# Four edits to a gated delta rule beside a stream of fp32 matmuls: a shorter inversion on VectorE, decay masks ahead of the exponential, two scalings given to ScalarE

## The chip, the cores and the metric

One core of a Trainium2 chip. The metric is the device time of one execution in microseconds (us); the time before is the median of three runs, 1537.29 us (1536.48 to 1538.0). The kernel's engines appear under the names of the profile: PE is TensorE (PEld its weight loads), DVE is VectorE, ACT is ScalarE, POOL is GpSimd, SP is the engine whose queue issues most transfers.

## The reference, cut to what matters

One decoder layer on 256 tokens of width 2048, all in fp32. After an RMSNorm, one wide input projection makes q, k, v, z, gates and a pooled branch. The part that the change touches is the gated delta rule, with 16 heads of 128 columns:

```
g = cumsum(g);  decay[i,j] = exp(g_i - g_j) for j <= i, else 0
lmat = strictly lower part of (beta_i k_i . k_j) * decay;  amat = lmat + I
u, w = solve(amat, [beta v, beta k exp(g)])        # unit lower triangular
o = (q decayed) . state + ((q . k) * decay) . (u - w . state);  state updated per chunk
o = rmsnorm(o) * gdn_norm_w * silu(z)
mixed = sigmoid(g_a) * o + sigmoid(g_b) * y_b;  x = x + mixed @ w_out
```

After that follow another RMSNorm, a gated MLP with a causal convolution (width 5632), a residual and a final RMSNorm. The kernel takes chunks of 128 tokens, two of them (t = 0, 1), in place of the reference's 64; the result is the same function.

## The kernel before, in words

**The weight stream.** Nearly all time goes into products of 256 tokens with weights that come from HBM in pieces of 128x1024 fp32 (512 KB). Each piece is loaded by SP into one of four `raw` buffers, rounded to fp32r by ACT (`whi`, line 317, in `begin`), and its rest is made by DVE (`wlo = raw - whi`, line 328). Three buffers each hold `whi` and `wlo`; `weights()` asks for pieces two ahead (`AHEAD = 2`). In `gemm_a` (lines 365 to 367) each piece feeds 12 matmuls: three products (high by high, low by high, high by low) for two 128-row parts and two token halves. So ACT, DVE and PE each run in a fixed order of their own; a late cast or split holds PE, and a PE that still reads an old piece holds the next cast.

**The groups.** The heads are worked in four groups g of four heads. For each group PE does the projections k, q, v, pool input, gate b, z, gate a and a small pool product. Beside them runs the delta rule of the group, `gdn` (lines 860 to 1093), a Python generator: `side()` is called after each 6 matmuls of a gemm and advances it by one `yield`, so that its instructions are emitted between those of the gemm. A scheduler then orders the instructions of each engine by its own model of their times; `tc.issue_after` adds an order, and inside `manual_schedule` PE keeps exactly the order of emission. Such a block (`fixed_order`) begins with the fourth group's gate a, and the small matmuls of its delta rule start behind six of the eight pieces there (`ending`); the block lasts through the first 12 pieces of the output projection.

**Inside `gdn`**, in order:

- `crow` (lines 871 to 874): the cumulated log decays of four heads as rows, brought to all 128 partitions by a DMA. `differences` (line 879): for each head and chunk one DVE instruction subtracts the partition's own value (`cumc`) and takes the minimum with 0. ACT takes the exponential (line 888, two heads at once), and POOL clears the entries below the diagonal (`affine_select`, line 890). The result is `dec0`, `dec1`.
- Grams (lines 901 to 925): for two heads at a time PE makes k.k and q.k products in PSUM (`pg0`, `pg1`); DVE takes the norms from the diagonal (line 906) and writes the products, scaled by `sj` and the decays, to `ga0` and `ga1`; the half of `pg0` that belongs to the next chunk is scaled by `sj` and `tail` (line 923).
- The inversion (lines 957 to 976): the 32x32 diagonal blocks of `lmat` go through DRAM (`cdd`, lines 939 and 942) so that 128 partitions hold 32 blocks times four parts `cq`; the inverse `tb` is 8 columns per partition (`idb` is the identity cut that way, line 635). For j = 0 to 30 DVE multiplies column j of the block by entry j of all 8 columns (line 965) and subtracts (line 967), over rows j+1 to 31. The result goes back through DRAM (`tbd`, written at line 972 and read at line 975) into `TTa`, and DVE transposes it (line 987). Larger blocks are built by small matmuls (line 1011 on).
- Output: w, the state and the outputs `po[0]` (PSUM) and `po[1]` (line 1079, in `vt`), their mean squares (lines 1085 and 1086), and the factor `ro` (lines 1088 to 1091, with a power on POOL).

**`gated`** (lines 1208 to 1216), after `gdn`: DVE multiplies both outputs by the gate `sz` (line 1211, 128x512 each), then eight instructions of 128x128 scale by `ro` and add `yb` (line 1215). `mixed` turns `sz` on PE (line 410) and makes `mhi` and `mlo` for the output projection. For groups 0 to 2 the scheduler places these transposes; for group 3 (`end`, after line 1240) they stand at a fixed place: four `side()` calls, so 24 matmuls, behind the point where `gated` is emitted.

Of the kernel before, what the change touches and what calls it, by code (L numbers as in the profile page):

```python
# [27 lines left out]
B0 = 32  # L28
NR = P // B0
AHEAD = 2  # L30
WAIT = 5
LATE = (26, 24, 22, 18)


@with_exitstack
def kernel(
# [20 lines left out]
    nc = tc.nc  # L57
# [5 lines left out]
    dpool = ctx.enter_context(tc.tile_pool(name="dram", bufs=2, space=bass.MemoryType.DRAM))  # L63
# [5 lines left out]
    def nm(s):  # L69
        cnt[0] += 1  # L70
        return f"{s}_{cnt[0]}"
# [561 lines left out]
    for cq in range(4):  # L633
        pr = slice(32 * cq, 32 * cq + 32)
        nc.gpsimd.affine_select(idb[pr], ones[pr, 0:1].unsqueeze(2).to_broadcast([32, 8, B0]),
                                pattern=[[-1, 8], [1, B0]], compare_op=ALU.is_equal, fill=0.0, base=-8 * cq,
                                channel_multiplier=0)


# [69 lines left out]
    nc.vector.tensor_scalar(mid, tri, tri[:, 63:64], None, op0=ALU.subtract)  # L709
    crs = mp.tile([NH, 2, P], F32, name="crs")  # L710
    crd = dpool.tile([4, 4 * S], F32, tag="crd", bufs=1, name="crd")
    cumc = mp.tile([P, 2, NH], F32, name="cumc")
    tail = mp.tile([P, NH], F32, name="tail")
    head = mp.tile([P, NH], F32, name="head")
    nhead = mp.tile([P, NH], F32, name="nhead")
# [1 line left out]
    def running_sums():  # L717
        pcr = pg([NH, 2, P])
        for t in range(2):
            mm(pcr[:, t, :], glog[:, t, :], mid, start=True, stop=True)  # L720
        nc.vector.tensor_copy(crs, pcr)
        nc.sync.dma_start(crd.rearrange("g (h s) -> (g h) s", h=4), crs.rearrange("h t i -> h (t i)"))
        yield
        pcc = pg([P, 2, NH])
        for t in range(2):
            nc.tensor.transpose(pcc[:, t, :], crs[:, t, :], ident[:NH, :NH])
        nc.vector.tensor_copy(cumc, pcc)

# [131 lines left out]
    def gdn(g, kq, vt, conv, res):  # L860
# [3 lines left out]
        ssk = mp.tile([P, 2, 4], F32, tag="ssk", name=nm("ssk"))  # L864
        nk = mp.tile([P, 2, 4], F32, tag="nk", name=nm("nk"))
        sj = mp.tile([P, 2, 4], F32, tag="sj", name=nm("sj"))
        dec0 = mp.tile([P, 4, P], F32, tag="dec0", name=nm("dec0"))
        dec1 = mp.tile([P, 4, P], F32, tag="dec1", name=nm("dec1"))

# [3 lines left out]
            nc.sync.dma_start(crow.rearrange("p h t i -> p (h t i)"), crd[g].partition_broadcast(P))  # L873
        yield

        def differences(hp):
            for h in (2 * hp, 2 * hp + 1):
                for t in range(2):
                    nc.vector.tensor_scalar(crow[:, h, t, :], crow[:, h, t, :],
                                            cumc[:, t, 4 * g + h : 4 * g + h + 1], 0.0,  # L880
                                            op0=ALU.subtract, op1=ALU.min)

        differences(0)
        yield
        for hp in range(2):
            hs = slice(2 * hp, 2 * hp + 2)
            for t, dec in ((0, dec0), (1, dec1)):
                nc.scalar.activation(dec[:, hs, :], crow[:, hs, t, :], AF.Exp)
            for d in (dec0[:, hs, :], dec1[:, hs, :]):
                nc.gpsimd.affine_select(d, d, pattern=[[0, 2], [1, P]], compare_op=ALU.is_ge, fill=0.0, base=0,  # L890
                                        channel_multiplier=-1)
            if hp == 0:
                differences(1)
            yield
        for hp in range(2):
            h0 = 2 * hp
# [14 lines left out]
            nc.gpsimd.tensor_tensor(nk[:, :, hs], ssk[:, :, hs], half.to_broadcast([P, 2, 2]), op=ALU.pow)  # L911
            nc.vector.reciprocal(sj[:, :, hs], ssk[:, :, hs])
            nc.vector.tensor_tensor(sj[:, :, hs], sj[:, :, hs], beta[:, :, 4 * g + h0 : 4 * g + h0 + 2], op=ALU.mult)
            for h in (h0, h0 + 1):
                pg0, pg1 = grams[h - h0]
                own, next_half = slice(0, P), slice(P, S)
                hh = 4 * g + h
                ga0h = ga0[:, h, :].rearrange("p (a s) -> p a s", a=2)
                pg0h = pg0.rearrange("p (a s) -> p a s", a=2)
                nc.vector.scalar_tensor_tensor(ga0h[:, :, own], pg0h[:, :, own], sj[:, 0, h : h + 1],  # L920
                                               dec0[:, h, :].unsqueeze(1).to_broadcast([P, 2, P]),
                                               op0=ALU.mult, op1=ALU.mult)
                nc.vector.tensor_scalar(ga0h[:, :, next_half], pg0h[:, :, next_half], sj[:, 0, h : h + 1],
                                        tail[:, hh : hh + 1], op0=ALU.mult, op1=ALU.mult)
                nc.vector.scalar_tensor_tensor(ga1[:, h, :].rearrange("p (a s) -> p a s", a=2),
                                               pg1, sj[:, 1, h : h + 1],
                                               dec1[:, h, :].unsqueeze(1).to_broadcast([P, 2, P]),
                                               op0=ALU.mult, op1=ALU.mult)
                yield
# [31 lines left out]
        with tc.issue_after(last_split[0]):  # L961
            nc.vector.tensor_copy(tb, idb)
        for j in range(B0 - 1):
            tv = tmp[:, :, j + 1 :]
            nc.vector.tensor_tensor(tv, lb[:, j, j + 1 :].unsqueeze(1).to_broadcast([P, 8, B0 - 1 - j]),
                                    tb[:, :, j : j + 1].to_broadcast([P, 8, B0 - 1 - j]), op=ALU.mult)
            nc.vector.tensor_tensor(tb[:, :, j + 1 :], tb[:, :, j + 1 :], tv, op=ALU.subtract)
            if j % 3 == 2:
                yield
        tbd = dpool.tile([32, 4, 8 * B0], F32, tag="tbd", name=nm("tbd"))  # L970
        for cq in range(4):
            nc.sync.dma_start(tbd[:, cq], tb[32 * cq : 32 * cq + 32].rearrange("p c i -> p (c i)"))
        for r in range(NR):
            rs = slice(B0 * r, B0 * (r + 1))
            nc.sync.dma_start(TTa[rs, :, rs], tbd.rearrange("(q r) a (c i) -> r (a c) q i", q=8, i=B0)[r])
        yield

        for _ in conv:
# [111 lines left out]
        for t in range(2):  # L1090
            nc.vector.tensor_scalar(ro[:, t, :], ro[:, t, :], rsq[:, t : t + 1], None, op0=ALU.mult)
        yield
        res.append((po, ro))

    for g in range(4):
        kq = mp.tile([P, 4, 2, S], F32, tag="kq", bufs=1, name=nm("kq"))
# [14 lines left out]
        res = []  # L1111
# [94 lines left out]
        nc.vector.tensor_tensor(sz4, sz4, gwb.unsqueeze(1).to_broadcast([P, 8, P]), op=ALU.mult)  # L1206

        def gated(sz=sz, res=res, yb=yb):
            po, ro = res[0]
            for t in range(2):  # L1210
                nc.vector.tensor_tensor(sz[:, t, :], po[t].rearrange("p h d -> p (h d)"), sz[:, t, :], op=ALU.mult)
            for t in range(2):
                for h in range(4):
                    hs = slice(h * P, (h + 1) * P)
                    nc.vector.scalar_tensor_tensor(sz[:, t, hs], sz[:, t, hs], ro[:, t, h : h + 1], yb[:, t, hs],
                                                   op0=ALU.mult, op1=ALU.add)

        if g < 3:
            drain()
# [518 lines left out]
```

## Time and profile before

| what | value |
|---|---|
| runs | 1538.0, 1536.48, 1537.29 us; median 1537.29 |
| span of the profiled execution | 1536.8 us, mean granted TensorE clock 0.998 |
| mixer stage (groups 0 to 3) | about 50 to 766 us of the span |
| gated MLP and final norm | from there to the end |
| 512 KB weight pieces loaded by SP from `w_in` | 224, median 4.3 us from issue to landing |

A row of the profile's groups gives line, engine, operation, output and inputs, shape, count, then busy us, the mean ns of one instruction, and the engine's idle time just ahead of it with what ended it. A row of the timeline gives start, duration in us, engine, line and a count where several are merged. Successive instructions of one engine overlap by part of their duration. A matmul of 512 columns is drawn 0.39 us long, while the next begins after 0.23 us.

### The profile page before, as it was taken

How to read it: one execution, taken by the hardware profiler on the slowest of the kernel's cores; microseconds unless marked ns; L12 is line 12 of the kernel's file. 1: busy time of each engine (PE TensorE's matmuls, PEld its weight loads, DVE VectorE, ACT ScalarE, POOL GpSimd, SP SyncE). 2: the span in 40 equal slices, each digit the busy share in tenths (PEclk: the TensorE clock that was granted, in tenths of full speed). 3: DMA queues.
4: the chain of work that ended last, by engine and by line, in shares of the span. 5: the costliest groups of instructions: out<-in, count | busy, mean ns of one | idle time of the engine just before them, and what ended most of it. 6: DMA issues, size and time to landing. Idle time of an engine off the chain costs nothing. (4 is left out here: it accounts for less than half of the span.)

```text
span 1536.8 us, 20233 instructions
## 1 busy us (share of the span) xinstructions
PE 1524.3 (99%) x7290; PEld 1255.4 (82%) x7290; DVE 1268.3 (83%) x1793; ACT 853.1 (56%) x1070; POOL 80.9 (5%) x105
## 2 busy tenths in 40 slices
PE   9999999999999999999999999999999999999997
PEld 8887888787878888788888888788888888888876
DVE  6788859896589858887567899999999886889896
ACT  6455446454455445454455666666666665555553
POOL 1010002000100000000000000000000011010200
PEclk9999999999999999999999999999999999999999
DMA  8776757776576766776588556656457478566662
GB/s 276 209 229 198 203 165 207 218 216 185 148 250 201 208 169 194 231 195 186 171 263 305 179 178 219 219 206 206 154 165 243 127 238 266 172 223 207 235 201 98
DMA packets 166515, 313.62 MB, mean 204 GB/s; under 512 B 19554, under 2 KB 23426, under 8 KB 166286
## 3 DMA queue, kind: packets, MB, share of 16 engines
q1 hardware_dynamic: 157280, 283.17, 59.2%
q0 software_dynamic: 7344, 27.27, 5.5%
q10 hardware_dynamic: 1790, 1.89, 0.4%
q8 instruction: 57, 0.93, 0.3%
q14 instruction: 44, 0.36, 0.1%
HBM read 303.33 MB, written 8.95 MB: 203 GB/s over the span
## 5 line engine op out<-in xcount | busy, mean ns | idle before, releaser
L317 ACT CAST whi<-raw 128x1024 fp32r<-128x1024 f32 x420 | 441.2, 1052 | 427.1 <-PE psm L366 270.0
L328 DVE TENSOR_TENSOR wlo<-raw,whi 128x1024 fp32r<-128x1024 f32 x418 | 507.7, 1220 | 146.0 <-ACT whi L317 140.2
L317 ACT CAST whi<-quad 128x1024 fp32r<-128x1024 f32 x182 | 190.5, 1053 | 136.8 <-PE psg L1418 43.5
L328 DVE TENSOR_TENSOR wlo<-quad,whi 128x1024 fp32r<-128x1024 f32 x182 | 220.0, 1219 | 30.0 <-ACT whi L317 29.4
L367 PE MATMUL psm<-wlo,xhl 128*128 128x512 f32 x432 | 169.5, 393 | 1.3 <-DVE wlo L328 1.2
L365 PE MATMUL psm<-whi,xhl 128*128 128x512 f32 x432 | 169.0, 391 | 0.0
L366 PE MATMUL psm<-whi,xhl 128*128 128x512 f32 x432 | 168.6, 390 | 0.0
L1418 PE MATMUL psg<-whi,fhl 128*128 128x512 f32 x504 | 127.2, 390 | 0.0
L1418 PEld LDWEIGHTS psg<-whi,fhl 128*128 128x128 f32 x504 | 94.5, 188 | 19.6
L367 PEld LDWEIGHTS psm<-wlo,xhl 128*128 128x128 f32 x432 | 81.1, 188 | 18.8 <-DVE wlo L328 2.2
L366 PEld LDWEIGHTS psm<-whi,xhl 128*128 128x128 f32 x432 | 81.1, 188 | 16.8
L365 PEld LDWEIGHTS psm<-whi,xhl 128*128 128x128 f32 x432 | 81.1, 188 | 16.7
L244 DVE TENSOR_TENSOR quad<-quad,quad 128x1024 f32<-128x1024 f32 x72 | 87.6, 1216 | 0.0
L1418 PE MATMUL psg<-wlo,fhl 128*128 128x512 f32 x252 | 69.9, 389 | 0.0
L1418 PE MATMUL psg<-whi,ups 128*128 128x512 f32 x216 | 58.9, 394 | 0.0
L1418 PEld LDWEIGHTS psg<-wlo,fhl 128*128 128x128 f32 x252 | 47.3, 188 | 9.9
L1403 PE MATMUL psm<-whi,hhi 128*128 128x512 f32 (+1 forms) x140 | 54.5, 389 | 0.1
L1403 PE MATMUL psm<-whi,hlo 128*128 128x512 f32 (+1 forms) x140 | 54.1, 386 | 0.0
L1403 PE MATMUL psm<-wlo,hhi 128*128 128x512 f32 (+1 forms) x140 | 54.0, 387 | 0.0
L365 PE MATMUL psm<-whi,mhi 128*128 128x512 f32 x128 | 50.8, 397 | 0.0
L367 PE MATMUL psm<-wlo,mhi 128*128 128x512 f32 x128 | 50.0, 390 | 0.0
L366 PE MATMUL psm<-whi,mlo 128*128 128x512 f32 x128 | 49.9, 390 | 0.0
(435 smaller groups left out, 2953.7 us busy)
## 6 DMA issues: line engine op xcount, KB each, us to landing
raw<-in_w_in_dram SPq DMA_DIRECT2D x224, 512.0 KB, 4.3
raw<-in_w_up_dram SPq DMA_DIRECT2D x104, 512.0 KB, 4.8
quad<-in_w_up_dram SPq DMA_DIRECT2D x72, 512.0 KB, 5.0
raw<-in_w_down_dram SPq DMA_DIRECT2D x56, 512.0 KB, 5.1
raw<-in_w_out_dram SPq DMA_DIRECT2D x32, 512.0 KB, 4.2
quad<-in_w_down_dram POOLq DMA_DIRECT2D x32, 512.0 KB, 5.3
mv<-vrow SPq DMA_DIRECT2D x12, 512.0 KB, 4.8
taps<-in_conv_qkv_w_dram SPq DMA_DIRECT2D x16, 256.0 KB, 6.6
```

Of the source, the lines that this page charges most:

```text
L244: nc.vector.tensor_tensor(out_, plus_, minus_, op=ALU.subtract)
L317: last_cast[0] = nc.scalar.copy(hi, raw).ins
L328: last_split[0] = nc.vector.tensor_tensor(lo, raw, hi.bitcast(F32), op=ALU.subtract).ins
L365: mm(ps[:, t, :], lh(k, t), hi[:, kk, :], start=(k == 0), stop=False)
L366: mm(ps[:, t, :], ll(k, t), hi[:, kk, :], start=False, stop=False)
L367: mm(ps[:, t, :], lh(k, t), lo[:, kk, :], start=False, stop=(k == nk - 1))
L1403: mm(ps[:, cs], lhs(kk), part_[:, kk, cs], start=(first and kk == 0 and n == 0), stop=(last and kk == 1 and n == 2), skip_group_check=shared)
L1418: mm(ps, lhs(kk), w[n][:, kk], start=(first and n == 0 and kk == 0 and lhs is high), stop=False, skip_group_check=True)
```

## The change

Four edits, all in the mixer stage:

1. **Inversion.** The columns of the inverse are spread over the four parts in another way: column 4m + cq instead of 8cq + m. Before step j only columns up to j are non-zero, so the two DVE instructions of step j take n = j // 4 + 1 of the 8 columns instead of all. `tbd` is laid out anew, `[32, 8, 4, 32]`; each of its four writes now has 256 pieces of 128 bytes where it had 32 of 1024 bytes; reads keep pieces of 128 bytes.
2. **Decays.** The eight DVE subtractions of `differences` go. POOL sets the masked entries of `crow` to -1e30 (`later_rows`, one select of 128x512 for two heads) ahead of the exponential, and ACT subtracts inside the exponential through its bias (`ncum`, the negative of `cumc`), one instruction for each head and chunk: eight of 128x128 instead of four of 128x256. The four selects of 128x256 behind the exponential go.
3. **Grams.** The next-chunk half of `pg0` is scaled by ACT instead of DVE, by `st` = `sj` * `tail`, which DVE makes for two heads at once.
4. **Output norm.** In `gated` ACT scales the outputs by `ro`, eight instructions of 128x128 into `vt`; then DVE multiplies by `sz` and adds `yb`, one instruction of 128x1024 each.

```
+NEVER = -1e30
...
-                                pattern=[[-1, 8], [1, B0]], compare_op=ALU.is_equal, fill=0.0, base=-8 * cq,
+                                pattern=[[-4, 8], [1, B0]], compare_op=ALU.is_equal, fill=0.0, base=-cq,
...
-        nc.vector.tensor_copy(cumc, pcc)
+        nc.vector.tensor_scalar(ncum, pcc, -1.0, None, op0=ALU.mult)
...
-        def differences(hp):
-            for h in (2 * hp, 2 * hp + 1):
-                for t in range(2):
-                    nc.vector.tensor_scalar(crow[:, h, t, :], crow[:, h, t, :],
-                                            cumc[:, t, 4 * g + h : 4 * g + h + 1], 0.0,
-                                            op0=ALU.subtract, op1=ALU.min)
+        def later_rows(hp):
+            d = crow[:, 2 * hp : 2 * hp + 2].rearrange("p h t i -> p (h t) i")
+            nc.gpsimd.affine_select(d, d, pattern=[[0, 4], [1, P]], compare_op=ALU.is_ge, fill=NEVER, base=0,
+                                    channel_multiplier=-1)
...
-            for t, dec in ((0, dec0), (1, dec1)):
-                nc.scalar.activation(dec[:, hs, :], crow[:, hs, t, :], AF.Exp)
-            for d in (dec0[:, hs, :], dec1[:, hs, :]):
-                nc.gpsimd.affine_select(d, d, pattern=[[0, 2], [1, P]], compare_op=ALU.is_ge, fill=0.0, base=0,
-                                        channel_multiplier=-1)
+            for h in (2 * hp, 2 * hp + 1):
+                for t, dec in ((0, dec0), (1, dec1)):
+                    nc.scalar.activation(dec[:, h, :], crow[:, h, t, :], AF.Exp,
+                                         bias=ncum[:, t, 4 * g + h : 4 * g + h + 1])
...
+            nc.vector.tensor_tensor(st[:, hs], sj[:, 0, hs], tail[:, 4 * g + h0 : 4 * g + h0 + 2], op=ALU.mult)
...
-                nc.vector.tensor_scalar(ga0h[:, :, next_half], pg0h[:, :, next_half], sj[:, 0, h : h + 1],
-                                        tail[:, hh : hh + 1], op0=ALU.mult, op1=ALU.mult)
+                nc.scalar.activation(ga0h[:, :, next_half], pg0h[:, :, next_half], AF.Copy, scale=st[:, h : h + 1])
...
-            tv = tmp[:, :, j + 1 :]
-            nc.vector.tensor_tensor(tv, lb[:, j, j + 1 :].unsqueeze(1).to_broadcast([P, 8, B0 - 1 - j]),
-                                    tb[:, :, j : j + 1].to_broadcast([P, 8, B0 - 1 - j]), op=ALU.mult)
-            nc.vector.tensor_tensor(tb[:, :, j + 1 :], tb[:, :, j + 1 :], tv, op=ALU.subtract)
+            n = j // 4 + 1
+            tv = tmp[:, :n, j + 1 :]
+            nc.vector.tensor_tensor(tv, lb[:, j, j + 1 :].unsqueeze(1).to_broadcast([P, n, B0 - 1 - j]),
+                                    tb[:, :n, j : j + 1].to_broadcast([P, n, B0 - 1 - j]), op=ALU.mult)
+            nc.vector.tensor_tensor(tb[:, :n, j + 1 :], tb[:, :n, j + 1 :], tv, op=ALU.subtract)
...
-        tbd = dpool.tile([32, 4, 8 * B0], F32, tag="tbd", name=nm("tbd"))
+        tbd = dpool.tile([32, 8, 4, B0], F32, tag="tbd", name=nm("tbd"))
         for cq in range(4):
-            nc.sync.dma_start(tbd[:, cq], tb[32 * cq : 32 * cq + 32].rearrange("p c i -> p (c i)"))
+            nc.sync.dma_start(tbd[:, :, cq, :], tb[32 * cq : 32 * cq + 32])
...
-            for t in range(2):
-                nc.vector.tensor_tensor(sz[:, t, :], po[t].rearrange("p h d -> p (h d)"), sz[:, t, :], op=ALU.mult)
             for t in range(2):
                 for h in range(4):
-                    hs = slice(h * P, (h + 1) * P)
-                    nc.vector.scalar_tensor_tensor(sz[:, t, hs], sz[:, t, hs], ro[:, t, h : h + 1], yb[:, t, hs],
-                                                   op0=ALU.mult, op1=ALU.add)
+                    nc.scalar.activation(vt[:, t, h, :], po[t][:, h, :], AF.Copy, scale=ro[:, t, h : h + 1])
+            nc.vector.tensor_tensor(sz, sz, vt.rearrange("p t h d -> p t (h d)"), op=ALU.mult)
+            nc.vector.tensor_tensor(sz, sz, yb, op=ALU.add)
```

More of the change, by code (lines that the diff above doesn't have):

```diff
@@ L711 @@
     crd = dpool.tile([4, 4 * S], F32, tag="crd", bufs=1, name="crd")
-    cumc = mp.tile([P, 2, NH], F32, name="cumc")
+    ncum = mp.tile([P, 2, NH], F32, name="ncum")
     tail = mp.tile([P, NH], F32, name="tail")
@@ L866, in gdn @@
         sj = mp.tile([P, 2, 4], F32, tag="sj", name=nm("sj"))
+        st = mp.tile([P, 4], F32, tag="st", name=nm("st"))
         dec0 = mp.tile([P, 4, P], F32, tag="dec0", name=nm("dec0"))
@@ L874, in gdn @@
         yield
-        def differences(hp):
-            for h in (2 * hp, 2 * hp + 1):
-                for t in range(2):
-                    nc.vector.tensor_scalar(crow[:, h, t, :], crow[:, h, t, :],
-                                            cumc[:, t, 4 * g + h : 4 * g + h + 1], 0.0,
-                                            op0=ALU.subtract, op1=ALU.min)
-        differences(0)
+        def later_rows(hp):
+            d = crow[:, 2 * hp : 2 * hp + 2].rearrange("p h t i -> p (h t) i")
+            nc.gpsimd.affine_select(d, d, pattern=[[0, 4], [1, P]], compare_op=ALU.is_ge, fill=NEVER, base=0,
+                                    channel_multiplier=-1)
+        later_rows(0)
         yield
         for hp in range(2):
-            hs = slice(2 * hp, 2 * hp + 2)
-            for t, dec in ((0, dec0), (1, dec1)):
-                nc.scalar.activation(dec[:, hs, :], crow[:, hs, t, :], AF.Exp)
-            for d in (dec0[:, hs, :], dec1[:, hs, :]):
-                nc.gpsimd.affine_select(d, d, pattern=[[0, 2], [1, P]], compare_op=ALU.is_ge, fill=0.0, base=0,
-                                        channel_multiplier=-1)
+            for h in (2 * hp, 2 * hp + 1):
+                for t, dec in ((0, dec0), (1, dec1)):
+                    nc.scalar.activation(dec[:, h, :], crow[:, h, t, :], AF.Exp,
+                                         bias=ncum[:, t, 4 * g + h : 4 * g + h + 1])
             if hp == 0:
-                differences(1)
+                later_rows(1)
             yield
@@ L916, in gdn @@
                 own, next_half = slice(0, P), slice(P, S)
-                hh = 4 * g + h
                 ga0h = ga0[:, h, :].rearrange("p (a s) -> p a s", a=2)
@@ L963, in gdn @@
         for j in range(B0 - 1):
-            tv = tmp[:, :, j + 1 :]
-            nc.vector.tensor_tensor(tv, lb[:, j, j + 1 :].unsqueeze(1).to_broadcast([P, 8, B0 - 1 - j]),
-                                    tb[:, :, j : j + 1].to_broadcast([P, 8, B0 - 1 - j]), op=ALU.mult)
-            nc.vector.tensor_tensor(tb[:, :, j + 1 :], tb[:, :, j + 1 :], tv, op=ALU.subtract)
+            n = j // 4 + 1
[3 more added lines that the diff above has]
+            nc.vector.tensor_tensor(tb[:, :n, j + 1 :], tb[:, :n, j + 1 :], tv, op=ALU.subtract)
             if j % 3 == 2:
                 yield
-        tbd = dpool.tile([32, 4, 8 * B0], F32, tag="tbd", name=nm("tbd"))
+        tbd = dpool.tile([32, 8, 4, B0], F32, tag="tbd", name=nm("tbd"))
         for cq in range(4):
-            nc.sync.dma_start(tbd[:, cq], tb[32 * cq : 32 * cq + 32].rearrange("p c i -> p (c i)"))
+            nc.sync.dma_start(tbd[:, :, cq, :], tb[32 * cq : 32 * cq + 32])
         for r in range(NR):
             rs = slice(B0 * r, B0 * (r + 1))
-            nc.sync.dma_start(TTa[rs, :, rs], tbd.rearrange("(q r) a (c i) -> r (a c) q i", q=8, i=B0)[r])
+            nc.sync.dma_start(TTa[rs, :, rs], tbd.rearrange("(q r) m a i -> r (m a) q i", q=8)[r])
         yield
@@ L1092, in gdn @@
         yield
-        res.append((po, ro))
+        res.append((po, ro, vt))
     for g in range(4):
@@ L1208, in gated @@
         def gated(sz=sz, res=res, yb=yb):
-            po, ro = res[0]
-            for t in range(2):
-                nc.vector.tensor_tensor(sz[:, t, :], po[t].rearrange("p h d -> p (h d)"), sz[:, t, :], op=ALU.mult)
+            po, ro, vt = res[0]
             for t in range(2):
                 for h in range(4):
-                    hs = slice(h * P, (h + 1) * P)
-                    nc.vector.scalar_tensor_tensor(sz[:, t, hs], sz[:, t, hs], ro[:, t, h : h + 1], yb[:, t, hs],
-                                                   op0=ALU.mult, op1=ALU.add)
+                    nc.scalar.activation(vt[:, t, h, :], po[t][:, h, :], AF.Copy, scale=ro[:, t, h : h + 1])
+            nc.vector.tensor_tensor(sz, sz, vt.rearrange("p t h d -> p t (h d)"), op=ALU.mult)
+            nc.vector.tensor_tensor(sz, sz, yb, op=ALU.add)
         if g < 3:
```

## The prediction

> **What bounds the kernel now.** I read the page first: its span and the share of each engine.
>
> ```profile
> span 1536.8 us, 20233 instructions
> PE 1524.3 (99%) x7290; PEld 1255.4 (82%) x7290; DVE 1268.3 (83%) x1793; ACT 853.1 (56%) x1070; POOL 80.9 (5%) x105
> ```
>
> PE is idle for 12.5 us in all. The change touches only the mixer, so I read that stretch alone (columns: start and end, length, then busy us of PE, PEld, DVE, ACT, POOL, the clock, the DMA share, GB/s), and then all that matmuls waited for.
>
> ```profile
> 50.00:766.00 716.00, 714.35 (x3585) 585.62 (x3584) 566.85 (x1018) 350.28 (x463) 38.50 (x32) 1.00 0.68 199
> ...
> PE psm L367 <- DVE wlo L328: 1.5, 2, 1.2
> PE psg L1418 <- DVE wlo L328: 1.2, 3, 0.8
> ```
>
> In 716 us PE is idle for 716 - 714.35 = 1.65 us, at a clock of 1.00. DVE is busy 79% of it and ACT 49%, so neither is the bound. The second wait, line 1418, lies in the MLP. But matmuls are drawn longer than their pitch, so a drawn idle time is too short, and I take the pitch from the chain of waits and the lost time from start to start in the timeline.
>
> ```profile
> 1261.49 34.04 PE psg L1418 x150
> ...
> 148.25 0.39 PE L366 MATMUL psm<-whi,xhl2b 128*128 128x512 f32 x1
> 148.95 0.50 PE L367 MATMUL psm<-wlo,xhl2b 128*128 128x512 f32 x1 [0.31 <-DVE wlo L328]
> ...
> 459.36 0.39 PE L366 MATMUL psm<-whi,xhl 128*128 128x512 f32 x1
> 460.95 0.50 PE L367 MATMUL psm<-wlo,xhl 128*128 128x512 f32 x1 [1.20 <-DVE wlo L328]
> ```
>
> The pitch is 34.04 / 150 = 0.227 us. The first wait costs 0.70 - 0.23 = 0.47 us, the second 1.59 - 0.23 = 1.36 us: 1.8 us that relief on DVE or ACT could give back in the whole mixer. No matmul is added or removed. This is the frame: whatever DVE saves, PE can be at most about 1.8 us earlier, 0.12%; what can move the time more is a new wait of PE.
>
> How much lateness PE forgives follows from the code and the pitch. Pieces are asked for two ahead in three buffers; 24 matmuls are 24 x 0.227 = 5.4 us, less a cast of 1.06 us and a split of 1.22 us (both rows stand further down, in group 3's timeline): about 3.2 us of cushion between a free buffer and a waiting PE.
>
> **The change, part by part.** The rows for it (busy us in all, then mean ns; four groups):
>
> ```profile
> L965 DVE TENSOR_TENSOR tmp<-lb,tb 128x248 f32<-128x248 f32 (+30 forms) x124 | 35.9, 290 | 7.8 <-DMA lb<-cdd 5.2
> L967 DVE TENSOR_TENSOR tb<-tb,tmp 128x248 f32<-128x248 f32 (+30 forms) x124 | 36.0, 290 | 3.0
> ...
> L965 DVE TENSOR_TENSOR tmp<-lb,tb 128x248 f32<-128x248 f32 x4 | 1.7, 417 | 5.2 <-DMA lb<-cdd 5.2
> L965 DVE TENSOR_TENSOR tmp<-lb,tb 128x8 f32<-128x8 f32 x4 | 0.7, 176 | 0.1
> ...
> L879 DVE TENSOR_SCALAR crow<-crow,cumc 128x128 f32<-128x128 f32 x32 | 7.4, 292 | 8.1 <-DMA crow<-crd 8.1
> L888 ACT ACTIVATE dec<-crow 128x256 f32<-128x256 f32 x16 | 6.0, 411 | 10.3 <-DVE crow L879 10.1
> L890 POOL TENSOR_SCALAR_AFFINE_SELECT dec<-dec x16: 404/409/5902, 80.9 to 596.8; 128x256 f32<-128x256 f32 x16
> ...
> L923 DVE TENSOR_SCALAR ga<-psg,sj,tail 128x256 f32<-128x256 f32 x16 | 8.5, 532 | 0.0
> L1211 DVE TENSOR_TENSOR sz<-vt,sz 128x512 f32<-128x512 f32 x4 | 2.8, 693 | 0.1
> L1211 DVE TENSOR_TENSOR sz<-psg,sz 128x512 f32<-128x512 f32 x4 | 2.7, 680 | 0.0
> L1215 DVE SCALAR_TENSOR_TENSOR sz<-sz,ro,yb 128x128 f32<-128x128 f32 x32 | 9.3, 360 | 0.0
> ...
> 144.25 2.45 ACT L982 ACTIVATE vt<-vt,nk 128x128 f32<-128x128 f32 x8 [0.95 <-DVE vt L822]
> 743.55 1.14 ACT L1068 ACTIVATE vt<-psg,head 128x128 f32<-128x128 f32 x4 [1.45 <-PE psg L1066]
> ```
>
> *Inversion.* Each step's width is n(31 - j) instead of 8(31 - j); summed over j it falls from 3968 to 1560. An element costs (417 - 176) / 240 = 1.0 ns, so two instructions a step save 2 x 2408 x 1.0 ns = 4.8 us a group, of (35.9 + 36.0) / 4 = 18.0; the 62 fixed costs of about 0.17 us stay. DVE saves 19 us in all, and none of it is on PE's path, since PE stood idle for 1.65 us; what hides it is the weight stream. The one place where I book a gain is the wait at 148 us. ACT's eight scalings of line 982 stand there ahead of a cast, and they waited for a `vt` that DVE made between inversion steps. Two or three of these, early ones of about 0.4 us, take 1 column of 8 and fall to about 0.2, so the scalings start some 0.5 us sooner: -0.5 us. The wait at 459 us has no inversion near it; I leave it.
>
> *Its DMAs.* Bounds for the write of `tbd` in 128-byte pieces come from the two nearest rows.
>
> ```profile
> cdd<-ga SPq DMA_DIRECT2D x32, 16.0 KB, 1.5
> tbd<-tb SPq DMA_DIRECT2D x16, 32.0 KB, 3.2
> ...
> 714.69 1.84 DVE L987 STREAM_TRANSPOSE T<-TT 32x256 f32<-32x256 f32 x4 [2.21 <-DMA TT<-tbd]
> 717.09 0.59 PE L1011 MATMUL psg<-T,ga 32*32 32x32 f32 x25
> ```
>
> `cdd` is written in 128-byte pieces already and lands 1.5 us after issue with half the bytes; `tbd` lands after 3.2. So I expect 1.5 to 3.2 us, no later than now, and at worst twice the first row. Behind these writes SP holds the four reads and the next weight loads; in group 3 PE's fixed order leaves 717.09 - (714.69 + 1.84) = 0.56 us after DVE's transposes. The inversion ends up to 4.8 us sooner, so I book 0. [...]
>
> *Decays.* DVE loses 7.4 / 4 = 1.9 us a group. ACT goes from four instructions of 0.41 us to eight at the spacing of line 982, 2.45 / 8 = 0.31: 2.45 against about 1.6, +0.8 us a group. POOL does two selects of twice the size, 0.82 us each by the median. The order matters more. POOL's select stood behind the exponential, and the Grams need it tens of us later. Now it stands between the DMA of `crow` and ACT, and behind ACT's exponentials queue the casts, for which PE waits. DVE no longer waits for that DMA (8.1 us). The bounds for one select are 0.82 us and, by the longest row, 5.9 us; I take 0.82, since 409 ns is the median. 0.82 us is inside the cushion: 0.
>
> *Grams.* DVE gives up 8.5 / 4 = 2.1 us a group and gains two instructions of 0.18; ACT takes four of 128x256, by line 888 0.41 us each, so 1.6 us a group. They are spread over several yields and hidden by the cushion: 0.
>
> *Output norm.* DVE: (2.8 + 2.7 + 9.3) / 4 = 3.7 us become two instructions of 128x1024, 2 x 1.22 = 2.4. ACT gains eight scalings, four from PSUM (1.14 us) and four from SBUF (half of 2.45): 2.4 us. In groups 0 to 2 the scheduler places the transposes that need the result, and it will place them later; the burst is inside the cushion. In group 3 the place is fixed. There the chain is on PE's path once its slack is gone:
>
> ```profile
> 749.35 0.68 DVE L1211 TENSOR_TENSOR sz<-psg,sz 128x512 f32<-128x512 f32 x1
> ...
> 755.11 0.35 DVE L1091 TENSOR_SCALAR ro<-ro,rsq 128x4 f32<-128x4 f32 x2
> 755.38 2.19 DVE L1215 SCALAR_TENSOR_TENSOR sz<-sz,ro,yb 128x128 f32<-128x128 f32 x8
> 757.48 1.22 DVE L328 TENSOR_TENSOR wlo<-raw,whi 128x1024 fp32r<-128x1024 f32 x1
> ...
> 755.60 1.06 ACT L317 CAST whi<-raw 128x1024 fp32r<-128x1024 f32 x1 [1.67 <-PE psm L366]
> ...
> 759.72 1.03 PE L410 MATMUL psg<-ident,sz 128*128 128x128 f32 x8
> ```
>
> Now `sz` is ready at 755.38 + 2.19 = 757.57, 2.15 us before its transposes. After the change: `ro` at 755.46, scalings 2.4, two DVE instructions 2.4, some 0.1 of hand-overs: 760.4, so PE waits 0.6 us. If ACT first does the cast that becomes free at 755.60, add 1.06: 1.7. If a split slips between DVE's two, add 1.2: 2.9. If the chain ahead runs sooner, because line 1211 no longer stands in front of `po[1]`, take off up to 1.4: then there is no wait. Between 0 and 2.9 I take the middle of the two likeliest, 1.1 us.
>
> **The sum.** -0.5 + 0 + 0 + 0 + 1.1 = +0.6 us on the span of 1536.8: 1537.4. The median of the runs stands 1537.29 - 1536.8 = 0.5 above that span: **1537.9 us**. DVE would drop by 4.8 + 1.9 + 1.7 + 1.3 = 9.7 us a group, 39 of 567 us in the mixer; ACT would rise by 0.8 + 1.6 + 2.4 = 4.8 us a group, 19 on 350.
>
> **The rivals.**
>
> *Relief reaches PE.* With DVE lighter, both waits of the mixer go and group 3 ends without one: -1.8 us, 1535.5. For it: both waits name DVE's split. Against it: the larger one stands where DVE runs convolution work that the change leaves alone. If the MLP's 1.2 us went too, through a shifted order of DVE, it would be 1534.3; nothing there is edited.
>
> *POOL is held and takes ACT with it (slower).* The longest select is this one:
>
> ```profile
> 237.94 7.12 POOL L890 TENSOR_SCALAR_AFFINE_SELECT dec<-dec 128x256 f32<-128x256 f32 x4 [1.53 <-ACT dec L888]
> ...
> 238.48 2.18 DVE L1215 SCALAR_TENSOR_TENSOR sz<-sz,ro,yb 128x128 f32<-128x128 f32 x8
> 240.59 3.49 DVE L328 TENSOR_TENSOR wlo<-raw,whi 128x1024 fp32r<-128x1024 f32 x3
> 243.99 0.47 DVE L839 SCALAR_TENSOR_TENSOR cy<-psg,cqw,cy 128x255 f32<-128x255 f32 x1
> ```
>
> Four selects of 0.41 us took 7.12, and one took 5.9: POOL stood while DVE ran eleven instructions that read two SBUF operands back to back, and went on at 244, when DVE turned to PSUM. Harmless then; after the change ACT waits behind it. It decides from a select late by more than the 3.2 us of cushion. At 5.9 us PE waits 2.7 us; with ACT's new scalings (2.4 us) in the same queue, at the same place (both follow the end of a group), up to 5.1. One such event of about 4 us on top of the forecast gives 1541.9. Against it: the median select took 409 ns, and DVE's eight instructions in `gated` become two that first wait for ACT, which leaves gaps. [...]
>
> *Nothing happens.* The scheduler orders the engines anew, the small waits change places, and the sum is 1537.3.
>
> **How the numbers follow.** A measurement of this kernel can tell about 0.2%, 3.1 us, from no change. Forecast, with its own range of 1536.3 (no wait in group 3) to 1539.7 (2.9 us there): 0.50. Nothing happens: 0.15. Relief: 0.18, of which 0.04 beyond 3.1 us. POOL holds ACT: 0.17, nearly all beyond +3.1 us (1540.4). So faster 0.04, same 0.79, slower 0.17. The range takes in relief down to 1535.2 and half of the POOL case, to 1541.0.
>
> **What would show it.** Right: line 410 of group 3 preceded by a wait of PE for DVE's `sz` of 0.6 to 1.7 us; DVE busy 528 and ACT 369 us in 50 to 766; casts of ACT that wait for PE as before. Wrong: ACT's exponentials waiting for POOL by 3 us or more, with a PE wait for `wlo` right after (the POOL case); all PE waits in the mixer gone (relief); a PE wait at line 1011 of group 3 (the DMAs). A time below 1534.2 would say that PE's order hides more lost time than its start-to-start rows show.

## The result, and the profile after

| | before | after |
|---|---|---|
| median of 11 runs | 1537.57 us (1536.48 to 1538.4) | 1540.13 us (1539.12 to 1542.15) |
| ratio after / before | | 1.0017, 95% interval 1.0009 to 1.0025 |
| span of the profiled execution | 1536.8 us | 1537.4 us, in a run of 1539.14 us |

The change costs 2.6 us. That lies inside 0.2%, and 2.2 us above the predicted time: inside the stated range (1535.2 to 1541.0), but above the forecast's own part of it, which ended at 1539.7. The first lines of the page and the mixer's stretch, columns as before:

```profile
span 1537.4 us, 20209 instructions
...
PE 1524.0 (99%) x7290; PEld 1255.8 (82%) x7290; DVE 1233.4 (80%) x1721; ACT 872.4 (57%) x1134; POOL 71.7 (5%) x97
```

```profile
50.00:766.00 716.00, 713.33 (x3581) 585.13 (x3580) 531.99 (x945) 369.28 (x527) 29.38 (x24) 1.00 0.67 199
```

The work moved as forecast: in the mixer DVE fell from 566.85 to 531.99 us (528 were forecast), and ACT rose from 350.28 to 369.28 (369). DVE's 35 us bought nothing: PE's idle time rose from 1.65 to 2.67 us. What PE waited for most, in the whole kernel (columns: us in total, times, longest):

```profile
PE psg L411 <- DVE sz L1212: 2.6, 1, 2.6
PE psg L1414 <- DVE wlo L329: 1.1, 3, 0.6
```

The waits for `wlo` on the gemm's line (367 before, 368 now) are gone from the list. In their place stands one wait, for `sz`, at the transposes of the last group. (Lines after the change are shifted by one to four: 411 is the 410 of before, 1211 and 1212 are the new DVE lines of `gated`, 1210 its ACT line.) The timeline around it:

```profile
753.27 0.36 DVE L1089 TENSOR_SCALAR ro<-ro,rsq 128x4 f32<-128x4 f32 x2
...
753.76 1.05 ACT L318 CAST whi<-raw 128x1024 fp32r<-128x1024 f32 x1 [1.67 <-PE psm L367]
...
754.72 1.13 ACT L1210 ACTIVATE vt<-psg,ro 128x128 f32<-128x128 f32 x4
...
755.73 1.28 ACT L1210 ACTIVATE vt<-vt,ro 128x128 f32<-128x128 f32 x4
...
757.04 1.23 DVE L1211 TENSOR_TENSOR sz<-sz,vt 128x1024 f32<-128x1024 f32 x1 [0.97 <-ACT vt L1210]
...
757.64 0.39 PE L368 MATMUL psm<-wlo,mhi 128*128 128x512 f32 x1
758.19 1.22 DVE L329 TENSOR_TENSOR wlo<-raw,whi 128x1024 fp32r<-128x1024 f32 x1
759.32 1.22 DVE L1212 TENSOR_TENSOR sz<-sz,yb 128x1024 f32<-128x1024 f32 x1
...
760.60 1.09 PE L411 MATMUL psg<-ident,sz 128*128 128x128 f32 x8 [2.56 <-DVE sz L1212]
```

Read it as a relay. `ro` is ready at 753.63. ACT takes up a cast first (1.05 us), then the eight scalings (until 757.01). DVE multiplies, does another piece's split (758.19), and only then adds. PE's last gemm matmul starts at 757.64, so by the pitch the transposes could start at 757.87; they start at 760.60. PE lost 2.73 us.

Both ends of that wait stand 1.8 us earlier than before, when `ro` was ready at 755.46 and the transposes started at 759.72: this execution has none of the earlier waits on the gemm's line. So the two profiled spans compare as 1536.8 - 1.85 + 2.73 = 1537.7, against 1537.4 measured.

The other edits, by the groups and the transfers, and for `crow` by the list of its instructions (ns as least, median, longest) and ACT's waits:

```profile
L965 DVE TENSOR_TENSOR tb<-tb,tmp 128x60 f32<-128x60 f32 (+24 forms) x124 | 26.0, 209 | 3.1
L963 DVE TENSOR_TENSOR tmp<-lb,tb 128x60 f32<-128x60 f32 (+24 forms) x124 | 25.9, 209 | 8.8 <-DMA lb<-cdd 5.9
```

```profile
tbd<-tb SPq DMA_DIRECT2D x16, 32.0 KB, 3.4
```

```profile
L880 POOL TENSOR_SCALAR_AFFINE_SELECT crow<-crow x8: 628/635/1617, 79.6 to 593.6; 128x512 f32<-128x512 f32 x8
```

```profile
ACT dec L888 <- POOL crow L880: 6.3, 5, 2.9
```

The inversion fell from 71.9 to 51.9 us, 5.0 a group. The small-piece write lands after 3.4 us instead of 3.2. A select of POOL takes 0.64 us where 0.82 was forecast, the longest 1.6, and ACT waits for POOL 2.9 us at the longest, inside the 3.2 us of cushion. In all ACT stood idle 6.3 us there; before, it stood 10.1 us ahead of the same exponentials, for DVE's subtractions, which waited for the same DMA.

### The profile page after: what moved, and what is told of

It is laid out like the page before. It is cut to its first block, busy times and chain, and to the rows that moved or that the text cites. A ratio compares the mean times of both kernels' runs of the same rounds, so it can differ in the third digit from the quotient of the medians.

```text
span 1537.4 us, 20209 instructions
## 1 busy us (share of the span) xinstructions
PE 1524.0 (99%) x7290; PEld 1255.8 (82%) x7290; DVE 1233.4 (80%) x1721; ACT 872.4 (57%) x1134; POOL 71.7 (5%) x97
```

## The experiments

Theory: the change's whole price is PE's wait in group 3, because PE's order is fixed there and the chain from `ro` to `sz` got longer. Rivals: the price sits elsewhere, in the new order of the casts and splits, or in POOL standing ahead of ACT. Times are medians of 11 runs unless the text says otherwise; each ratio is against runs of the kernel before on the same chip. "Of after" means edits made to the changed kernel.

### Group 3 finished the old way

```
+            if g == 3:
+                for t in range(2):
+                    nc.vector.tensor_tensor(sz[:, t, :], po[t].rearrange("p h d -> p (h d)"), sz[:, t, :], op=ALU.mult)
+                for t in range(2):
+                    for h in range(4):
+                        hs = slice(h * P, (h + 1) * P)
+                        nc.vector.scalar_tensor_tensor(sz[:, t, hs], sz[:, t, hs], ro[:, t, h : h + 1], yb[:, t, hs],
+                                                       op0=ALU.mult, op1=ALU.add)
+            else:
...
```

> All four edits, but in group 3 alone the output norm is done in the old way (two DVE products of 128x512, eight DVE instructions of 128x128). Theory (the wait of 2.7 us that PE now has ahead of group 3's transposes is the whole loss, and the waits for wlo that went, about 2.1 us, are a real gain): no wait of PE at these transposes, 1540.1 - 2.7 = 1537.4 us, ratio to the kernel before 0.999 to 1.000. Rival (the loss lies outside that wait, in runs that differ from the profiled one or in time around the span): 1539.3 us or more, the wait gone and the time still 1.5 us or more above the kernel before.

Measured: 1536.44 us, ratio 0.9995 (0.9986 to 1.0004). The mixer's stretch and the place in the timeline:

```profile
50.00:766.00 716.00, 715.40 (x3590) 586.76 (x3589) 533.76 (x953) 367.41 (x518) 28.87 (x24) 1.00 0.68 200
```

```profile
754.03 2.18 DVE L1214 SCALAR_TENSOR_TENSOR sz<-sz,ro,yb 128x128 f32<-128x128 f32 x8
...
758.36 1.03 PE L411 MATMUL psg<-ident,sz 128*128 128x128 f32 x8
```

`sz` is ready at 756.21 and PE does not wait for it. One group's `gated` put back takes 3.7 us off, all of the change's price; the 0.6 us that the median lies below the kernel before are inside the interval. DVE keeps nearly its whole relief (534 us), so the relief is not what costs. The profiled execution is the longest of the eleven (1538.91 us): its span, 1537.2, is hardly below after's, but the time went elsewhere, most of it in the MLP, where the change edits nothing. So the 3.7 us rest on the medians, and the trace shows only that the wait is gone.

### Transposes moved by two calls, later and earlier

Later:

```
         gated()
-        for _ in range(4):
+        for _ in range(6):
```

> All four edits, and group 3's transposes stand 12 matmuls (two side steps, 12 x 0.227 = 2.7 us) later in PE's fixed order. Theory: the wait shrinks from 2.7 us to under 0.3, time 1537.4 to 1537.8 us. Rival (the chain of sz is paced by what PE does, so that it moves along with the transposes; or the loss lies elsewhere): a wait of 1 us or more is left, or the time stays at 1539 us or more.

Measured: 1539.8 us, ratio 1.0013 (1.0004 to 1.0022); against 1540.13 hardly less. The expectation was missed. The timeline says why:

```profile
759.01 0.39 PE L368 MATMUL psm<-wlo,mhi 128*128 128x512 f32 x1
759.33 1.22 DVE L1212 TENSOR_TENSOR sz<-sz,yb 128x1024 f32<-128x1024 f32 x1
760.60 0.86 PEld L411 LDWEIGHTS psg<-ident,sz 128*128 128x128 f32 x8 [1.63 <-DVE sz L1212]
...
761.93 0.73 PE L366 MATMUL psm<-whi,mhi 128*128 128x512 f32 x2 [0.24 <-ACT mhi L1225]
...
762.66 0.19 PEld L367 LDWEIGHTS psm<-whi,mlo 128*128 128x128 f32 x1 [0.43 <-DVE mlo L1226]
```

The last matmul before the transposes starts at 759.01 instead of 757.64: six matmuls later, not twelve, since the pieces in which such calls stand run out and the rest of the emission is drained at once. `sz` is ready at the same instant, 760.60, so the chain stayed as it was when the transposes moved back, and the wait shrinks to 760.60 - 759.01 - 0.23 = 1.36 us. Then the gemm that needs `mhi` and `mlo` follows the transposes at once, and PE waits for both, about 0.8 us together. Counted to the same gemm matmul behind them, PE is 0.6 us ahead of after's trace; the spans differ by 0.2 us and the medians by 0.3.

Earlier:

```
         gated()
-        for _ in range(4):
+        for _ in range(2):
```

> All four edits, and group 3's transposes stand two side steps (12 matmuls, 2.7 us) earlier in PE's fixed order. Theory (PE loses at that place one for one whatever its chain is late): the wait grows from 2.7 to 5.4 us, time 1540.1 + 2.7 = 1542.8 us. Rival (the wait is partly made up later, or the chain moves with PE): under 1541.5 us.

Measured: 1543.25 us (5 runs), ratio 1.0034 (1.0022 to 1.0047), 3.1 us above after. Its waits and two stretches (the clock is the third number from the end):

```profile
PE psg L411 <- DVE sz L1212: 4.3, 1, 4.3
```

```profile
756.00:760.00 4.00, 0.81 (x4) 0.81 (x5) 2.45 (x2) 0.62 (x3) 0.00 (x0) 0.87 0.40 135
760.00:762.00 2.00, 2.00 (x9) 1.81 (x8) 0.88 (x2) 1.17 (x2) 0.12 (x1) 0.50 0.00 0
762.00:764.00 2.00, 2.00 (x10) 1.60 (x9) 0.51 (x1) 1.05 (x1) 1.51 (x2) 0.91 0.21 39
```

The wait grows by 1.7 us, not by the expected 2.7: here no split stands between DVE's two instructions (they start at 756.65 and 757.91), and `sz` is ready 5.9 us after `ro` instead of 6.9. Something else comes with the wait: the granted clock falls to 0.50. The time lost to it is 4 x 0.13 + 2 x 0.50 + 2 x 0.09 = 1.7 us, as much as 3.4 us at half speed. In after's own profiled execution no such fall follows the wait of 2.73 us.

### Without the new output norm, and it alone

Of after, with `gated` as it was before (the other three edits stay):

```
-                    nc.scalar.activation(vt[:, t, h, :], po[t][:, h, :], AF.Copy, scale=ro[:, t, h : h + 1])
-            nc.vector.tensor_tensor(sz, sz, vt.rearrange("p t h d -> p t (h d)"), op=ALU.mult)
-            nc.vector.tensor_tensor(sz, sz, yb, op=ALU.add)
+                nc.vector.tensor_tensor(sz[:, t, :], po[t].rearrange("p h d -> p (h d)"), sz[:, t, :], op=ALU.mult)
...
+                    nc.vector.scalar_tensor_tensor(sz[:, t, hs], sz[:, t, hs], ro[:, t, h : h + 1], yb[:, t, hs],
+                                                   op0=ALU.mult, op1=ALU.add)
```

> Three edits: inversion, decays, Grams; the output norm of all groups as before. Theory: as with the old way in group 3 alone, 1537.4 us, since the ACT scalings of groups 0 to 2 cost nothing: within 0.5 us of that kernel. Rival (ACT's scalings in groups 0 to 2 delay casts as well): 0.5 us or more faster than that kernel.

Measured: 1539.01 us, ratio 1.0012 (1.0003 to 1.0021). The expectation was missed: with the new `gated` gone the loss should have gone too. There is indeed no wait at the transposes, but others have come. PE's waits, POOL's and ACT's timeline at 598 us, and an earlier place:

```profile
PE psm L368 <- DVE wlo L329: 1.7, 3, 0.7
```

```profile
598.23 1.23 POOL L880 TENSOR_SCALAR_AFFINE_SELECT crow<-crow 128x512 f32<-128x512 f32 x2 [17.52 <-DMA crow<-crd]
```

```profile
598.90 0.69 ACT L888 ACTIVATE dec<-crow,ncum 128x128 f32<-128x128 f32 x2 [4.40 <-POOL crow L880]
```

```profile
81.06 2.45 ACT L888 ACTIVATE dec<-crow,ncum 128x128 f32<-128x128 f32 x8 [3.31 <-POOL crow L880]
...
85.77 0.50 PE L368 MATMUL psm<-wlo,xhl 128*128 128x512 f32 x1 [0.53 <-DVE wlo L329]
```

Here the sign of the prediction's rival, ACT behind POOL by 3 us or more and then a wait of PE for `wlo`, appears twice: 3.31 us and then 0.53 at 85.77, 4.40 us and then 0.73 at 606.86. But DVE did not hold POOL; POOL had stood idle until the DMA of `crow` landed. The first place shows the same in the traces of two other kernels: with group 3 the old way ACT waits 3.66 us and PE 0.53, with the earlier load 3.19 and 0.41; in after, 2.89 us there are followed by no wait. So the cushion ends near 3 us, as estimated. These two waits are not the whole loss: PE comes to line 1011 at 718.78, 3.5 us later than in after's trace.

The reverse of that diff on the kernel before (the new `gated`, none of the other edits):

> The output norm's edit alone on the kernel before. Theory: group 3's wait of 1.5 to 2.9 us comes with this edit alone, and PE's waits for wlo at 148, 281 and 459 us stay, since the other edits removed them: 1539.1 to 1540.5 us, ratio 1.001 to 1.002. Rival (the loss comes from the sum of the four): under 1538.3 us.

Measured: 1544.14 us (5 runs), ratio 1.0049 (1.0037 to 1.0062). Alone, this edit costs 7.1 us (1537.07 before), nearly three times what all four cost together, and the expectation was missed by 3.6 us. PE's waits, and the stretches behind the first of them:

```profile
PE psg L410 <- DVE sz L1214: 2.6, 1, 2.6
PE psm L367 <- DVE wlo L328: 1.5, 2, 0.9
...
PE psg L1011 <- DVE T L987: 0.7, 1, 0.7
```

```profile
762.00:764.00 2.00, 1.01 (x5) 1.01 (x6) 0.93 (x1) 0.00 (x0) 0.00 (x0) 0.60 0.45 143
764.00:766.00 2.00, 2.00 (x9) 1.77 (x8) 1.08 (x2) 1.17 (x2) 0.33 (x1) 0.54 0.32 119
```

The same 2.6 us stand at the transposes, now with the clock at 0.60 and 0.54 in the two stretches behind them (2 x 0.40 + 2 x 0.46 = 1.7 us lost). And PE waits at line 1011 for DVE's transposes of the inverse, the place where 0.56 us of slack were counted before; from start to start it is 1.1 us late there. With the drawn 1.5 us for splits the parts come to 2.7 + 1.7 + 1.1 + 1.5 = 7.0 us, and this span (1541.3) is 7.0 us above that of the kernel before in its second trace (1534.3, below). In the full change DVE's transposes for line 1011 start at 707.55, where before they started at 714.69 and here at 716.27, and no wait follows: by these rows the shorter inversion pays there for what the new output norm costs.

### The decay rows loaded one group earlier

```
-        crow = mp.tile([P, 4, 2, P], F32, tag="crow", name=nm("crow"))
-        with tc.issue_after(last_load[0]):
-            nc.sync.dma_start(crow.rearrange("p h t i -> p (h t i)"), crd[g].partition_broadcast(P))
+        if g == 0:
+            load_crow(0)
+        crow = crows[g]
...
+        if g < 3:
+            load_crow(g + 1)
         q2 = kq[:, :, 1, :]
```

`load_crow` holds the removed lines; the second call stands behind the loads of `lb`, in the middle of group g.

> Inversion, decays and Grams, output norm as before, and the load of the decay rows is issued one group ahead (behind the inversion's loads), so that ACT's exponentials and POOL's select find them there. The same three edits without that took 1539.0 us, with ACT held 4.4 us behind POOL and the late rows in group 3 and waits of PE for wlo right after. Theory (the decays edit puts ACT's queue behind a load that lands late, and that is what these three edits pay): ACT's waits for POOL in groups 1 to 3 go, and the time falls by 1 to 2.5 us, to 1536.5 to 1538. Rival (another order of DVE and ACT, not the load): within 0.7 us of 1539.0.

Measured on the kernel without the new output norm: 1538.62 us, ratio 1.0007 (0.9998 to 1.0016), 0.4 us less, which is inside the noise; the expected 1 to 2.5 us did not come. ACT's waits for POOL did go, from 12.7 us in four places to 3.2 in one, group 0's, whose load was not moved. From PE's waits:

```profile
PE psm L368 <- DVE wlo L329: 2.8, 3, 1.3
```

PE still waits for splits, 2.8 us in this trace, at other places. So the late load was not the main loss there. The rival, that another order of the engines' work carries it, is left, argued and not shown; which instruction of that order does it is not settled.

> All four edits with group 3's output norm in the old way, and the decay rows loaded one group ahead. Without the early load 1536.4 us, and there ACT waited for POOL by 0.3 to 1.9 us a group in the profiled execution, inside the cushion of 3.2 us. Theory (late rows cost only beyond the cushion): 1535.5 to 1536.5 us, a narrower spread of the runs. Rival (the 512 KB moved beside the Grams holds up weight pieces there): 1537 us or more.

Measured on the kernel with group 3 the old way: 1536.21 us, ratio 0.9991 (0.9982 to 1.0000). The mixer's stretch:

```profile
50.00:766.00 716.00, 716.00 (x3597) 588.58 (x3596) 536.75 (x956) 368.73 (x520) 26.47 (x24) 1.00 0.68 200
```

PE is busy for 716.00 of 716 us: in this execution nothing was left to gain in the mixer by moving work off DVE. Time and spread came out as expected (1535.29 to 1537.01 us, where it was 1535.9 to 1538.91 without the early load). By its ratio this is the best version, and its interval still reaches 1.

### The kernel before, looked at again

No edit.

> The kernel before once more, for a second trace. Theory (the wait of 1.36 us at 459 us comes from a late load and not from the order, so it is not in every execution): PE's waits for wlo in the mixer sum to less than in the first trace, under 1.2 us against 2.1, and the span is 1534 to 1536 us against 1536.8. Rival: the same three waits, 2.0 us or more.

Measured: 1536.03 us (one run), span 1534.3. The mixer's stretch:

```profile
50.00:766.00 716.00, 716.00 (x3596) 588.03 (x3595) 568.35 (x1019) 351.88 (x464) 38.09 (x32) 1.00 0.68 200
```

The same program, and PE is busy 716.00 of 716 us where the first profile had 714.35. The mixer's waits of the first profile belonged to that execution; not every one has them.

This trace is the cleanest to measure the change against. From the first small matmul of line 1011 (1009 after the change) to the transposes PE keeps a fixed order, the same in both kernels. Here are both ends in this trace, then the first in after's; its second, 760.60, stands further up.

```profile
714.80 0.69 PE L1011 MATMUL psg<-T,ga 32*32 32x32 f32 x32
...
757.42 1.03 PE L410 MATMUL psg<-ident,sz 128*128 128x128 f32 x8
```

```profile
715.26 0.69 PE L1009 MATMUL psg<-T,ga 32*32 32x32 f32 x32
```

The stretch takes 757.42 - 714.80 = 42.62 us here, as in the first profile (759.72 - 717.09 = 42.63) and with group 3 the old way (758.36 - 715.74 = 42.62). After the change it takes 760.60 - 715.26 = 45.34, with the product ahead of the factor (next) 758.02 - 714.80 = 43.22. So of the 3.1 us by which after's span exceeds this one, 2.7 arise in this stretch, and they are the wait.

### The product ahead of the factor

```
+            if g == 3:
+                for t in range(2):
+                    nc.vector.tensor_tensor(sz[:, t, :], po[t].rearrange("p h d -> p (h d)"), sz[:, t, :], op=ALU.mult)
+                for t in range(2):
+                    for h in range(4):
+                        hs = slice(h * P, (h + 1) * P)
+                        nc.scalar.activation(sz[:, t, hs], sz[:, t, hs], AF.Copy, scale=ro[:, t, h : h + 1])
+                nc.vector.tensor_tensor(sz, sz, yb, op=ALU.add)
+            else:
...
```

> All four edits, but in group 3 DVE multiplies by the gate before the factor is known, ACT scales that product, and only DVE's addition of 128x1024 stands behind the scalings. Theory (the chain behind the factor is the sum of cast, eight scalings, DVE's instructions and the split that slips between them): one DVE instruction of 1.2 us and the split's 1.15 leave the chain, the wait falls from 2.7 us to between 0 and 1.5, time 1537.5 to 1538.9 us. Rival (the wait comes from ACT's scalings as such, late behind casts): 2 us or more is left, 1539.5 us or more.

Measured: 1536.75 us, ratio 0.9997 (0.9988 to 1.0006). The place in the timeline:

```profile
754.26 2.45 ACT L1214 ACTIVATE sz<-sz,ro 128x128 f32<-128x128 f32 x8
756.75 1.22 DVE L1215 TENSOR_TENSOR sz<-sz,yb 128x1024 f32<-128x1024 f32 x1 [1.13 <-ACT sz L1214]
758.02 0.86 PEld L411 LDWEIGHTS psg<-ident,sz 128*128 128x128 f32 x8 [0.87 <-DVE sz L1215]
```

The two products need no `ro` and run ahead of it. ACT still does the eight scalings, but behind them there is one DVE instruction instead of two, and no split can slip between. The cast still goes first (753.31). The transposes start at 758.02 instead of 760.60, PE's wait is some 0.6 us, and 3.4 us come off after's time. So ACT can do the scaling; what costs most is a second DVE instruction behind it, with another stream's split in front: from `ro` to `sz` it takes 4.8 us here and 6.9 in after.

### The other edits one at a time

Each alone on the kernel before, with the hunks of edit 1, 2 or 3 of the diff shown with the change; the runs of the kernel before beside them have a median of 1537.38 us.

> The inversion's edit alone, with its layout. Theory (DVE's time is off PE's path, and small writes land no later): ratio to the kernel before 0.9985 to 1.001, no wait of PE for the inverse in group 3. Rival (DVE's relief reaches PE): 0.998 or less.

Measured: 1538.66 us, ratio 1.0010 (1.0001 to 1.0018). From PE's waits:

```profile
PE psm L367 <- DVE wlo L328: 1.2, 1, 1.2
...
PE psg L410 <- ACT ev L781: 0.8, 1, 0.8
```

An edit that takes 17 us off DVE (549.79 us in the mixer, from 566.85) makes the kernel 1.3 us slower, a loss that the interval only just tells from none. No wait stands at the inverse; in this trace two stand elsewhere, at 640 us (for a split) and at 242 us (for ACT). The order had changed near the first: group 3's Grams run at 618 to 632 us instead of 627 to 648. That the new order causes these waits is not shown.

> The decays' edit alone: POOL masks the rows ahead of ACT's exponentials. Theory (late rows hold ACT, mostly inside the cushion): 0.9995 to 1.001. Rival (ACT's queue behind POOL is a price by itself): 1.001 or more, with waits of PE for wlo just behind ACT's waits for POOL.

Measured: 1536.13 us, ratio 0.9993 (0.9984 to 1.0002). The moved select costs nothing that can be measured.

> The Grams' edit alone: the next-chunk half scaled by ACT. Theory: within 0.1% of the kernel before. Rival (ACT's copies stand ahead of casts and DVE waits for them in the same bank): 1.001 or more.

Measured: 1539.17 us, ratio 1.0006 (0.9997 to 1.0015). From PE's waits, and the stretches behind line 1011:

```profile
PE psg L1011 <- DVE T L987: 1.1, 2, 0.7
```

```profile
718.00:720.00 2.00, 2.00 (x30) 1.68 (x23) 1.90 (x6) 1.03 (x4) 0.00 (x0) 0.68 0.32 117
720.00:722.00 2.00, 2.00 (x7) 1.54 (x6) 0.00 (x0) 1.04 (x1) 0.00 (x0) 0.50 0.65 202
722.00:724.00 2.00, 2.00 (x10) 1.66 (x9) 1.91 (x2) 1.27 (x2) 0.00 (x0) 0.97 0.16 60
```

The median is not clear of no change, and the profiled execution is one of the longest (1540.58 us; the runs lie between 1536.63 and 1541.06). In it the slack at line 1011 is overrun again, and the clock falls behind it (2 x 0.32 + 2 x 0.50 + 2 x 0.03 = 1.7 us lost). The four parts alone come to about +1.3 - 1.3 + 1.8 + 7.1 = +8.9 us; together they cost 2.6. Line 1011 shows why such parts need not add up: they share slack there, and what one edit uses, another gives.

## Why the prediction was right, and where it was off

**The frame held.** PE is the bound, DVE's saving is hidden, and only a new wait of PE moves the time. DVE's and ACT's busy times came out within 1%. That the time fell inside the stated range is in part luck: its upper end, 1541.0, was there for the rival in which DVE holds POOL, which did not happen; the forecast with its own worst case ended at 1539.7.

**The wait in group 3: right mechanism, low end taken.** The prediction put PE's wait at the transposes between 0 and 2.9 us and took 1.1. It was 2.73, outside the 0.6 to 1.7 us named as the sign of being right, and for the reasons named for the upper end: ACT took the cast first, and a split slipped between DVE's two instructions. The two cases that it called likeliest, 0.6 and 1.7, both left the split out. The last term of the prediction, a chain that runs up to 1.4 us sooner, gave nothing here: `ro` came 1.8 us earlier, but so did PE. The wait's size was varied four ways, and the time went with it: 4.4 us of wait, 1543.25 (with 1.7 us of low clock); 2.7, 1540.13; 2.2 with later transposes (1.4, and 0.8 for `mhi` and `mlo`), 1539.8; 0.6, 1536.75; none, 1536.44. Between 2.2 and 0.6 the time drops by more than the wait does.

**The gain of 0.5 us was not there.** The wait at 148 us is gone from after's trace, and it is also gone from the second trace of before. A wait seen once was booked as if every execution had it. For the same reason the rival "relief reaches PE" had less to give than 1.8 us: in the second trace, nothing in the mixer.

**The step from span to median was wrong.** "0.5 above that span" set the profiled execution's span beside the median of other runs. In every run here, of both kernels, the device time is 1.7 us above that run's own span. So the profiled execution of before, at 1536.8, was a long one: it would be a run of 1538.5, and the eleven runs in the table end at 1538.4. After's profiled execution, at 1537.4, was among the shortest of its 11 (1537.4 to 1540.4, median 1538.4). The forecast span of 1537.4 was met by luck, by a base too long and a wait too short; the medians differ by 2.6 us, not by 0.6. The same 0.5 us is missing at the low end of the forecast's own range: with no wait in group 3 its sum gives 1536.8, not 1536.3.

**What stays open of the size.** The wait of 2.7 us covers the 2.6 us between the medians, whose interval runs from 1.4 to 3.8. But taking the wait out brought 3.4 to 3.7 us. The rest could be noise, or a fall of the clock in part of after's executions: the five shortest spans have a mean granted clock of 0.9988, the six longest, 1.8 us longer, 0.9978, and one stretch of 3.4 us at half speed is 1.7 / 1537 = 0.0011. Against it: the runs with later transposes fall into two groups as well (1537.5 to 1538.9, and 1539.8 to 1540.65), and their recorded clocks differ by 0.0001 only. There is no trace of a long execution of after, so this is argued and not shown. It could also be group 0's late rows, which cost 0.4 to 0.5 us where ACT waited longer than about 3.

**The zeros.** DMAs: right (3.4 us, no wait at line 1011 in after). Decays: right in after (longest wait of ACT for POOL 2.9 us, just inside the cushion) and alone (0.9993); ACT did stand behind POOL by more than 3 us in three other traces, at most 4.40, each time through the late DMA of `crow` and at 0.4 to 0.7 us for PE. Before the change ACT stood behind the same DMA, through DVE; the prediction's own row shows these 10.1 us, and it did not count them. Grams: no cost is seen beside the shorter inversion; alone they overran the 0.56 us at line 1011 in one trace. The rival "nothing happens" points at what is left over, small waits that change places with the order: 1.3 us with the inversion alone and 1.9 us without the new output norm, lost ahead of line 1011. That the order does it, and which instructions, stays open.

## What to carry to other kernels

Where one engine is 99% busy, price a change at the places where that engine's order is fixed, by the length of the chain that ends there: count every hand-over between engines, and at each one the instruction of another stream that may go first. Work taken off an engine that is not the bound was worth nothing by itself here (17 us off DVE in the mixer alone: ratio 1.0010), but it can lengthen or shorten such a chain, and edits that share slack do not add up. Before a wait of a fraction of a per cent is booked as a gain, look at a second execution, and compare a span with its own run's time only.

## What the runs showed of the hardware

**A short wait can cost twice.** Behind three waits of PE the granted clock fell: to 0.50 (760 to 762 us) behind one of 4.4 us, with the transposes moved earlier; to 0.54 (764 to 766) behind one of about 2.7 us, with the new output norm alone; to 0.50 (720 to 722) behind two of together about 1.4 us with small matmuls between them, with the Grams alone. Each time the stretches show about 1.7 us lost on top of the wait, as much as 3.4 us at half speed. It does not follow every such wait: behind the 1.1 us lost at the same small matmuls with the new output norm alone, the sum of 7.0 us above leaves no room for a second fall, and behind the wait of 2.73 us in after's profiled execution the clock stayed at 1.00, as this stretch shows:

```profile
760.00:762.00 2.00, 1.41 (x11) 1.32 (x12) 0.63 (x2) 0.71 (x2) 0.00 (x0) 1.00 0.65 210
```

So the length of the wait alone does not tell: about 2.7 us stands on both sides, and about 1.4 us was enough once. What decides it is not shown.

**POOL's selects were hardly late any more.** Before, the median select took 0.41 us and the longest 5.90; after, the median of the eight took 0.64 and the longest 1.62. With the decays alone, which move the selects, POOL was busy for 28.22 us in the mixer, where it was 38.50 before. With the new output norm alone, which leaves them where they were, it was 34.84, and the selects are these:

```profile
L890 POOL TENSOR_SCALAR_AFFINE_SELECT dec<-dec x16: 403/1012/1460, 80.2 to 595.6; 128x256 f32<-128x256 f32 x16
```

There the longest took 1.46 us. Nor was every select late that ran beside DVE instructions with two SBUF operands, as the one beside the eleven was; this one of the first trace of before was not:

```profile
416.40 2.33 DVE L1215 SCALAR_TENSOR_TENSOR sz<-sz,ro,yb 128x128 f32<-128x128 f32 x8
...
417.06 0.48 POOL L890 TENSOR_SCALAR_AFFINE_SELECT dec<-dec 128x256 f32<-128x256 f32 x1 [4.09 <-ACT dec L888]
```

It took 0.48 us inside eight such instructions of DVE. What made the difference is not shown.
